# Two product groups moved onto banks already in use, and one weight block scaled earlier, in the channel half of a decoder layer

## The chip, the cores and the metric

The kernel runs on one core of a Trainium2 chip. The metric is the device time of one execution in microseconds. Four engines compute: PE (TensorE, the matrix engine, with its weight loads shown as PEld), DVE (VectorE), ACT (ScalarE) and POOL (GpSimd). SP (SyncE) only issues transfers. PE writes its results into PSUM, eight banks of 128 x 512 float32, from where DVE and ACT read them; everything else lies in SBUF, and weights come by DMA from device memory.

## The reference

One decoder layer on 512 tokens of width 1024: two attention branches, then a gated MLP, each followed by a LayerNorm. The change lies in the MLP:

```python
u2 = x * (1.0 + sc2) + sh2
h = _causal_depthwise_conv(u2 @ w_up, conv_w, conv_b)
h_gate, h_val = jnp.split(h, 2, axis=-1)
ffn_out = (jax.nn.silu(h_gate) * h_val) @ w_down
x = _layer_norm(DEEPNORM_ALPHA * x + (1.0 + gt2) * ffn_out, ln2_g, ln2_b)
```

Here `x` is 512 x 1024, `w_up` 1024 x 5632, `w_down` 2816 x 1024, and `(1.0 + gt2)`, called the gate below, is one factor per output column.

## The kernel before

**Split products.** Every float32 operand is split into a high part (ACT rounds it) and a low part (DVE subtracts the high part). A product is three matmuls: high x high, high x low, low x high. For streamed weights the high part is `wh` and the low part `wl` (`split_proc`, three buffers each) or, in the down projection's other blocks, `wdh` and `wdl`. The subtraction is line 91, whatever it works for.

**Up projection** (loop at line 1099, n = 0 to 43). Each n streams a weight tile of 128 x 1024, multiplies it with all tokens into one bank in 24 matmuls (lines 133 to 135), and applies the convolution: one ACT operation (line 1124) and two on DVE (lines 1125 and 1126) that read the bank. Six of the eight banks are held by running sums from n = 7 on, so two rotate here. Two tiles make one gated hidden tile, two hidden tiles make a pair; there are FP = 11 pairs.

**Down projection.** It is computed by the Strassen-Winograd scheme with seven products instead of eight for 2 x 2 blocks. The tokens are cut into two halves of 256 (the first half is row blocks 0 and 1 of 128 tokens, the second row blocks 2 and 3), the 1024 output columns into two halves of 512, and a pair's two hidden tiles are the inner halves. `blocks` (line 1051) forms sums of the activations on DVE. The weights of a pair are B11, B12, B21, B22 (each 128 x 512), and their sums are built in `pair_proc` (line 940): a transfer that adds gives the tile `b`, which holds T1 = B11 + B12 and T3 = B12 + B22, and two additions on DVE give T2 and T4. `b` is stored to device memory (`t13`) for later, and B22 times the gate's right half is stored too (`wgt`, written from tile `g`; the gate isn't ready for pairs 0 and 1, whose B22 is loaded and scaled at n = 15 and 19 by `scale_proc`).

A product of a pair is six matmuls, three for each of two row blocks (`product`, lines 1076 to 1078), and sums over the 11 pairs in two banks. The seven products and their place:

- P1 (with B11), Y (T2) and Z2 (T4) are summed during the up projection, pair by pair, in the six held banks (`early_products`).
- Z (T3) and W1 (T1) come after it, in two new banks each (`phase`), weights loaded back from `t13`.
- X (B21) and then W (B22, scaled) follow, again in two new banks each. W's first three pairs use `wl` weights; its last eight (`LATE`) are split ahead into `wdh`/`wdl`. For row block 2 these eight are one piece of 512 columns (24 matmuls, the wide piece), for row block 3 two pieces of 256 columns (24 narrow matmuls each), so that row block 3 can be normalised sooner.

**From products to output.** Between the matmuls DVE combines the products, multiplies by the gate's half `g0` or `g1` and adds to the residual `r[i][e]` (row block i, column half e; tiles `xn`). `gated` (line 1155) is the last two of these steps. `z_mark`, `v_mark`, `x_mark` and `w_mark` are called after each weight tile of the stages Z, W1, X and W and hold this work. P1 is first copied by ACT into `p1`. `tail` normalises a row block (`ln_stats`, then two scalings per piece, lines 1169 and 1173) and stores it.

**Order.** SP's loads stand in the order in which the program is written. On PE, DVE, ACT and POOL a scheduler sets the order when the program is built; each engine then works its list strictly in order, and waits on the others through semaphores. Weight items are loaded up to five ahead (`weights`).

Of the kernel before, what the change touches and what calls it, by code (L numbers as in the profile page):

```python
# [37 lines left out]
AHEAD = 2  # L38
NSPLIT = 3
LATE = 8  # L40
EARLY = 2
GS = 9
SS = 10
# [7 lines left out]
def layer_kernel(ctx: ExitStack, tc: tile.TileContext, out, xT, x, cT, crow, wa0, wa1, bcol, bgt, w1, wct, wv, bf,  # L51
# [912 lines left out]

    wui, pi, wai = [], [], {}
# [9 lines left out]
    for n in range(2 * FT):  # L975
        wui.append(add_item(wup[n], split_proc))
        if n in GTILES:
            k = GTILES.index(n)
            wai[(10, 28)[k // 4]] = add_item(wa1[(28, 24)[k // 4] + k % 4], ada_proc((28, 24)[k // 4] + k % 4))
        if n in (15, 19):  # L980
            p = (15, 19).index(n)
            add_item(wdp[p][:, 1024:1536], scale_proc(p), 512)
# [92 lines left out]
    def product(ps, ah, al, bh, bl, first, last):  # L1075
        PE.matmul(ps, ah, bh, start=first, stop=False)  # L1076
        PE.matmul(ps, ah, bl, start=False, stop=False)  # L1077
        return PE.matmul(ps, al, bh, start=False, stop=last)  # L1078

    yz = []  # L1080

# [70 lines left out]
    def half(w, e):  # L1152
        return [t[:, e * 512 : (e + 1) * 512] for t in w]

    def gated(i, e, t, src, op=ALU.add):
        V.tensor_tensor(t, src, (g0, g1)[e], ALU.mult)
        V.tensor_tensor(r[i][e], r[i][e], t, op)


    def stat_tile():  # L1160
        return cons.tile([P, 3, 6], F32, name=nm("st"), tag="st3", bufs=2)
# [11 lines left out]
            V.scalar_tensor_tensor(v, v, rs, lnr[1][:, c], ALU.mult, ALU.add)  # L1173
            eng.dma_start(out[tb, c], v)

    p1, u2, q1, u3, c22 = [[fine(n) for _ in range(2)] for n in ("p1", "u2", "q1", "u3", "c22")]

    def phase(ps, idx, end, take, mark, last=None):
        for n, k in enumerate(idx):
            w = weights(k)  # L1180
            for a, p in enumerate(range(2 * n, min(end, 2 * n + 2))):
                t = take(p)
                for i in range(2):
                    product(ps[i], t[:, top[i]], t[:, bot[i]], *half(w, a), p == 0, p == FP - 1)
            mark(n)
        if end < FP:
            t = take(end)
# [11 lines left out]
    def z_mark(n):  # L1199
# [3 lines left out]
        if n == 2:  # L1203
            early_products(FP - 1)
        if n == 3:
            Y, Z2, P1 = yz
            for i in range(2):
                S.activation(p1[i], P1[i], AF.Copy)
            for i in range(2):
                V.tensor_tensor(u2[i], p1[i], Y[i], ALU.subtract)  # L1210
# [5 lines left out]
    def v_mark(n):  # L1216
        for p in range(max(SS, 2 * n), min(FP, 2 * n + 2)):
            ops[p][3] = halves(ops[p][3])
        if n == 0:
            for i in range(2):  # L1220
                V.tensor_tensor(q1[i], q1[i], Z[i], ALU.add)
                V.tensor_tensor(u3[i], u2[i], Z[i], ALU.add)
        if n in (1, 2):
            gated(n - 1, 0, q1[n - 1], q1[n - 1])

    def first_rows(i):
        st = stat_tile()
# [2 lines left out]
        tail(i, st, [(0, 0, 512), (1, 0, 512)], G)  # L1230

    def x_mark(n):
        if n == 0:
            for i in range(2):
                V.tensor_tensor(c22[i], u3[i], W1[i], ALU.add)
                V.tensor_tensor(u2[i], u2[i], W1[i], ALU.add)
# [33 lines left out]
    V.tensor_tensor(r[3][1], r[3][1], W[1], ALU.add)  # L1270
    for i in range(2):
        pieces = [(1, 0, 512)] if i == 0 else [(1, 0, 256), (1, 256, 512)]
        for n, (e, c0, c1) in enumerate(pieces):
            ps = bank()[:, 0 : c1 - c0] if i else W[0]
            for q in range(LATE):
                t = ops[FP - LATE + q][3]
                product(ps, t[:, top[i]], t[:, bot[i]], wc[q][0][:, c0:c1], wc[q][1][:, c0:c1], i == 1 and q == 0, q == LATE - 1)
            v = r[2 + i][e][:, c0:c1]
            V.tensor_tensor(v, v, ps, ALU.add)
            V.bn_stats(sts[i][:, n + 1, :], v)  # L1280
        tail(2 + i, sts[i], [(0, 0, 512)] + pieces, nc.sync)

# [70 lines left out]
```

## Time and profile before

| what | value |
| --- | --- |
| median of 3 runs | 755.78 us (755.17 to 755.9) |
| profiled execution, its own time | 754.3 us |
| span of its instructions | 752.5 us |
| up projection on PE, about | 390 to 674 us |
| stages Z, W1, X, W on PE, about | 674 to 741 us |
| DMA over the span | 169 GB/s |

A row of the timeline gives start and length in microseconds, the engine, the line, the operation, output and inputs, shapes, how often, and in brackets the idle time before it and what ended it. Operations on one engine overlap at their ends, so the distance between two starts is what an operation costs its engine, not its length. A list of waits gives total, number and longest. "SPq" and "ACTq" are those engines' issues of transfers.

### The profile page before, as it was taken

The numbers are of one execution on the slowest core, as the hardware profiler recorded it, in microseconds if no ns is written. First come the engines' busy times: TensorE is split into PE (matmuls) and PEld (weight loads), VectorE is DVE, ScalarE is ACT, GpSimd is POOL, SyncE is SP. The second block draws the span as 40 slices with busy tenths as digits, with TensorE's granted clock in tenths as the row PEclk, the third lists the DMA queues.
The fourth block names the chain that finished last, engine by engine and source line by source line (L and its number), as shares of the span: only waits on it lengthen the run. The fifth ranks groups of instructions, "written<-read, shape, count | busy, mean of one in ns | idle before, by whom it ended". The sixth has DMA issues, their size and how long they took to land.

```text
span 752.5 us, 9875 instructions
## 1 busy us (share of the span) xinstructions
PE 734.0 (98%) x3478; PEld 607.6 (81%) x3478; DVE 607.1 (81%) x1017; ACT 386.0 (51%) x678; POOL 109.0 (14%) x138
## 2 busy tenths in 40 slices
PE   8999999999999999999999999999999999999993
PEld 4878888878888888788889888888888888887883
DVE  6869799888788894765587889987696678769997
ACT  4566566685866564433065554454454355346530
POOL 1026223453010011453000000000000000000010
PEclk9999999999999999999999999999999999999997
DMA  8943446313422331542063778587874665557611
GB/s 331 405 175 116 164 169 214 122 58 112 169 92 83 108 112 62 195 168 84 1 240 77 252 243 275 161 250 223 253 213 165 187 218 151 171 182 264 220 63 57
DMA packets 43252, 128.01 MB, mean 170 GB/s; under 512 B 5665, under 2 KB 6177, under 8 KB 43202
## 3 DMA queue, kind: packets, MB, share of 16 engines
q1 hardware_dynamic: 37602, 112.09, 42.5%
q0 software_dynamic: 2576, 7.41, 5.2%
q10 hardware_dynamic: 3024, 7.88, 3.0%
q8 instruction: 27, 0.44, 0.2%
q14 instruction: 23, 0.19, 0.1%
HBM read 117.07 MB, written 10.22 MB: 169 GB/s over the span
## 4 chain that ended last, share of the span: by engine, by line
PE 82%; DVE 10%; DMA 3%; issue 2%; ACT 2%; POOL 0%; SPq 0%; DVEq 0%; ACTq 0%
PE ps L135 18%; PE ps L133 18%; PE ps L134 18%; PE ps L301 5%; PE ps L1077 3%; PE ps L1078 2%; PE ps L1076 2%; PE ps L552 2%; DVE wl L91 2%; PE ps L534 2%; PE ps L893 2%; PE ps L892 2%; PE ps L894 2%; PE ps L475 1%; PE ps L476 1%
## 5 line engine op out<-in xcount | busy, mean ns | idle before, releaser
L91 DVE TENSOR_TENSOR wl<-raw,wh 128x1024 fp32r<-128x1024 f32 (+2 forms) x112 | 139.2, 1244 | 53.9 <-ACT wh L182 53.5
L182 ACT ACTIVATE wh<-raw 128x1024 fp32r<-128x1024 f32 (+1 forms) x103 | 108.5, 1053 | 124.0 <-PE ps L134 59.8
L133 PE MATMUL ps<-u2h,wh 128*128 128x512 f32 (+1 forms) x376 | 141.6, 377 | 0.0
L135 PE MATMUL ps<-u2h,wl 128*128 128x512 f32 (+1 forms) x376 | 141.2, 376 | 0.0
L134 PE MATMUL ps<-u2l,wh 128*128 128x512 f32 (+1 forms) x376 | 141.2, 376 | 0.0
L133 PEld LDWEIGHTS ps<-u2h,wh 128*128 128x128 f32 x376 | 70.8, 188 | 13.6 <-issue 0.8
L135 PEld LDWEIGHTS ps<-u2h,wl 128*128 128x128 f32 x376 | 70.8, 188 | 12.8
L134 PEld LDWEIGHTS ps<-u2l,wh 128*128 128x128 f32 x376 | 70.8, 188 | 12.7
L133 PE MATMUL ps<-uh,wh 128*128 128x512 f32 x200 | 79.4, 397 | 0.0
L135 PE MATMUL ps<-uh,wl 128*128 128x512 f32 x200 | 78.3, 391 | 0.9 <-DVE wl L91 0.9
L134 PE MATMUL ps<-ul,wh 128*128 128x512 f32 x200 | 78.3, 391 | 0.0
L1124 ACT ACTIVATE cv<-ps,cw 128x512 f32<-128x512 f32 x44 | 33.9, 770 | 24.9 <-PE ps L135 19.0
L135 PEld LDWEIGHTS ps<-uh,wl 128*128 128x128 f32 x200 | 37.6, 188 | 9.5 <-DVE wl L91 1.3
L161 POOL DMA_DIRECT2D raw<-in_wdp x11 | 9.5, 867 | 244.1 <-DVE raw L947 95.0
L514 POOL TENSOR_TENSOR pt<-pt,om 128x127 f32<-128x127 f32 (+3 forms) x32 | 43.2, 1360 | 8.0 <-DVE om L513 8.0
L133 PEld LDWEIGHTS ps<-uh,wh 128*128 128x128 f32 x200 | 37.6, 188 | 7.4
L134 PEld LDWEIGHTS ps<-ul,wh 128*128 128x128 f32 x200 | 37.6, 188 | 7.2
L1125 DVE SCALAR_TENSOR_TENSOR cv<-ps,cw,cv 128x511 f32<-128x511 f32 x44 | 32.8, 745 | 9.1 <-ACT cv L1124 9.1
L1132 ACT ACTIVATE cv<-cv 128x512 f32<-128x512 f32 x22 | 13.9, 630 | 39.0 <-DVE cv L1126 38.9
L1126 DVE SCALAR_TENSOR_TENSOR cv<-ps,cw,cv 128x510 f32<-128x510 f32 x44 | 32.8, 745 | 0.2
L633 POOL TENSOR_TENSOR raw<-raw,gt 128x1024 f32<-128x1024 f32 x8 | 20.9, 2618 | 66.9 <-DMA raw<-in_wo 54.4
L513 DVE TENSOR_TENSOR_SCAN om<-om,dg 128x127 f32<-128x127 f32 (+3 forms) x32 | 29.6, 982 | 0.5 <-ACT om L508 0.4
(226 smaller groups left out, 1607.3 us busy)
## 6 DMA issues: line engine op xcount, KB each, us to landing
raw<-in_wup SPq DMA_DIRECT2D x44, 512.0 KB, 4.6
raw<-in_wa SPq DMA_DIRECT2D x32, 512.0 KB, 4.3
raw<-in_wct SPq DMA_DIRECT2D x25, 512.0 KB, 3.7
raw<-in_wdp SPq DMA_DIRECT2D x22, 512.0 KB, 5.7
wa<-in_wa SPq DMA_DIRECT2D x14, 512.0 KB, 7.9
raw<-in_wdp SPq DMA_DIRECT2D x22, 256.0 KB, 4.6
raw<-in_wdp POOLq DMA_DIRECT2D x11, 512.0 KB, 7.7
t<-raw ACTq DMA_DIRECT2D x10, 512.0 KB, 3.6
```

The costliest lines, as they stand in the source:

```text
L91: state["read"] = V.tensor_tensor(o, i, fl(hi), ALU.subtract)
L133: PE.matmul(ps, wh, ah, start=first, stop=False)
L134: PE.matmul(ps, wh, al, start=False, stop=False)
L135: return PE.matmul(ps, wl, ah, start=False, stop=last)
L182: state["hi"] = S.activation(h[:, 0:cols], r[:, 0:cols], AF.Copy)
L301: PE.matmul(grp[g], w, u, start=j == 0 and n == 0, stop=j == KT - 1 and n == (1 if g == 7 else 2))
L513: V.tensor_tensor_scan(d0, d0, dg[:, 513 - (e - s) : 512][:, ::-1], 0.0, ALU.mult, ALU.max)
L514: G.tensor_tensor(pt[b][:, s : e - 1], pt[b][:, s : e - 1], om[:, s + 1 : e], ALU.mult)
L1077: PE.matmul(ps, ah, bl, start=False, stop=False)
L1124: S.activation(t, ps, AF.Identity, bias=cw[:, n, 3:4], scale=cw[:, n, 2:3])
L1125: V.scalar_tensor_tensor(t[:, 1:], ps[:, 0:511], cw[:, n, 1:2], t[:, 1:], ALU.mult, ALU.add)
L1126: V.scalar_tensor_tensor(t[:, 2:], ps[:, 0:510], cw[:, n, 0:1], t[:, 2:], ALU.mult, ALU.add)
```

## The change

1. **X goes on in P1's banks.** X's first matmul no longer clears a bank (`fresh=False`); it adds to P1, which ACT has copied before. P1 + X is then in the bank as the sum that the left half of the second token half needs, and one addition per row block is dropped in `w_mark`.
2. **W goes on in W1's banks.** Since W carries the gate's right half, W1 has to carry it too: T1 is multiplied by it in `pair_proc` before it is stored (pairs 2 to 10), and for pairs 0 and 1 the stored T1 is loaded, scaled and stored again at n = 23 and 27. DVE subtracts W1 from the residual of row blocks 0 and 1 before W begins, and W1 + W from that of row blocks 2 and 3 at the end. The sign of one activation sum (`s4`) is turned.
3. **The combinations between are written anew**: 24 DVE operations of 128 x 512 instead of 30, more of them in stages Z and W1 (`z_mark`, `v_mark`), fewer in X and W (`x_mark`, `w_mark`).

```diff
@@ pair_proc
             w = wdc_proc(r)
+            if p > 1:
+                V.tensor_tensor(b[:, 0:512], b[:, 0:512], gt[1][:, 512:1024], ALU.mult)
             with tc.issue_after(state["last"].ins):
                 if p < FP - 1:
                     S.dma_start(t13[p], b)
@@
-    def scale_proc(p):
+    def scale_proc(dst):
         def f(r):
             V.tensor_tensor(r, r, gt[1][:, 512:1024], ALU.mult)
-            G.dma_start(wgt[p], r)
+            G.dma_start(dst, r)
@@
+        if n in (23, 27):
+            t = t13[(23, 27).index(n)][:, 0:512]
+            add_item(t, scale_proc(t), 512)
@@ blocks
-        V.tensor_tensor(s4, o[:, hi], e[:, lo], ALU.subtract)
+        V.tensor_tensor(s4, e[:, lo], o[:, hi], ALU.subtract)
@@ z_mark
             for i in range(2):
                 V.tensor_tensor(u2[i], p1[i], Y[i], ALU.subtract)
-                V.tensor_tensor(q1[i], u2[i], Z2[i], ALU.add)
+        if n in (4, 5):
+            fold(n - 2, 1, tm[n - 4], u2[n - 4], ALU.subtract)
@@ v_mark
-        if n == 0:
-            for i in range(2):
-                V.tensor_tensor(q1[i], q1[i], Z[i], ALU.add)
-                V.tensor_tensor(u3[i], u2[i], Z[i], ALU.add)
-        if n in (1, 2):
-            gated(n - 1, 0, q1[n - 1], q1[n - 1])
+        if n in (0, 1):
+            for a, b, c in zip((u3, q1)[n], (u2, u3)[n], (Z, Z2)[n]):
+                V.tensor_tensor(a, b, c, ALU.add)
+        if n in (2, 3):
+            fold(n - 2, 0, q1[n - 2], q1[n - 2])
+        if n in (4, 5):
+            fold(n - 4, 1, u3[n - 4], u3[n - 4], ALU.subtract)
@@ x_mark
-        if n == 0:
-            for i in range(2):
-                V.tensor_tensor(c22[i], u3[i], W1[i], ALU.add)
-                V.tensor_tensor(u2[i], u2[i], W1[i], ALU.add)
-        if n in (1, 2):
-            gated(n - 1, 1, c22[n - 1], c22[n - 1], ALU.subtract)
-        if n in (3, 4):
-            first_rows(n - 3)
-        if n == 4:
-            for i in range(2):
-                gated(2 + i, 1, u2[i], u2[i], ALU.subtract)
+        if n in ROWS:
+            i = ROWS.index(n)
+            V.tensor_tensor(r[i][1], r[i][1], W1[i], ALU.subtract)
+            first_rows(i)
@@
-    X = [bank() for _ in range(2)]
-    phase(X, xi, FP, lambda p: ops[p][1], x_mark)
-    W = [bank() for _ in range(2)]
+    phase(P1, xi, FP, lambda p: ops[p][1], x_mark, fresh=False)
@@ w_mark
-                V.tensor_tensor(p1[i], p1[i], X[i], ALU.add)
-                gated(2 + i, 0, p1[i], p1[i])
+                fold(2 + i, 0, p1[i], P1[i])
@@
-                product(W[i], t[:, top[i]], t[:, bot[i]], *half(w, a), p == 0, i == 1 and p == FP - LATE - 1)
+                product(W1[i], t[:, top[i]], t[:, bot[i]], *half(w, a), False, i == 1 and p == FP - LATE - 1, True)
@@
-            ps = bank()[:, 0 : c1 - c0] if i else W[0]
+            ps = bank()[:, 0 : c1 - c0] if i else W1[0]
@@
-            V.tensor_tensor(v, v, ps, ALU.add)
+            V.tensor_tensor(v, v, ps, ALU.subtract)
```

`fold` is `gated` under another name, `ROWS` is (3, 4), and `product` gets a flag that allows sums to go on in a used bank.

The scheduler also places some instructions elsewhere. First, the end of PE's list. Before, W's first two matmuls (banks 6826 and 6827) are followed by all 48 narrow ones (banks 6896 and 6923), and the list ends with 16 more of W and the 24 of the wide piece, whose last rows are these:

```order
L1077 MATMUL ps_6826<-wdl_6732,hv_6206 128x512
L1078 MATMUL ps_6826<-wdh_6731,hv_6206 128x512
L1076 MATMUL ps_6826<-wdh_6772,hv_6639 128x512
L1077 MATMUL ps_6826<-wdl_6773,hv_6639 128x512
L1078 MATMUL ps_6826<-wdh_6772,hv_6639 128x512
```

Now W is in banks 6536 and 6537 (those of W1). After W's first two matmuls come 15 narrow ones of bank 6903, then the 16 of W and the wide piece, which ends in the first rows here, and then the narrow ones that are left:

```order
L1082 MATMUL ps_6536<-wdh_6786,hv_6660 128x512
L1083 MATMUL ps_6536<-wdl_6787,hv_6660 128x512
L1084 MATMUL ps_6536<-wdh_6786,hv_6660 128x512
L1082 MATMUL ps_6903<-wdh_6720,hv_6014 128x256
L1083 MATMUL ps_6903<-wdl_6721,hv_6014 128x256
L1084 MATMUL ps_6903<-wdh_6720,hv_6014 128x256
```

So 9 matmuls of bank 6903 and 24 of bank 6930 moved from ahead of the wide piece to behind it; these three kinds of rows go on to the list's end.

Second, the end of DVE's list, where `xn_3625`/`xn_3626` are row block 2's column halves and `xn_3741`/`xn_3742` row block 3's. Before:

```order
L1270 TENSOR_TENSOR xn_3742<-xn_3742,ps_6827 128x512
L1279 TENSOR_TENSOR xn_3742<-xn_3742,ps_6896 128x256
L1279 TENSOR_TENSOR xn_3742<-xn_3742,ps_6923 128x256
L1280 BN_STATS st_6829<-xn_3742 128x6 x2
L1279 TENSOR_TENSOR xn_3626<-xn_3626,ps_6826 128x512
L1280 BN_STATS st_6828<-xn_3626 128x6
L854 BN_AGGR mv_6883<-st_6828 128x2
L854 BN_AGGR mv_6950<-st_6829 128x2
```

Now:

```order
L1276 TENSOR_TENSOR xn_3626<-xn_3626,ps_6536 128x512
L1277 BN_STATS st_6837<-xn_3626 128x6
L1276 TENSOR_TENSOR xn_3742<-xn_3742,ps_6903 128x256
L855 BN_AGGR mv_6890<-st_6837 128x2
L1277 BN_STATS st_6838<-xn_3742 128x6
L858 TENSOR_SCALAR mv_6890<-mv_6890 128x1
L859 RECIPROCAL mv_6890<-mv_6890 128x1
L1174 SCALAR_TENSOR_TENSOR xn_3625<-xn_3625,mv_6890,ln_0_5279 128x512
```

Row block 2 is added and normalised first, the four scalings of lines 1174 and 1178 included, and only then comes row block 3's second narrow piece (bank 6930) with its own normalisation.

Third, DVE's list in stage X. Before, two operations per row block read W1 near the stage's start:

```order
L91 TENSOR_TENSOR wdl_6679<-rl_6644,wdh_6678 128x512
L1235 TENSOR_TENSOR c_1178_6321<-u_1176_6319,ps_6517 128x512
L1236 TENSOR_TENSOR u_1172_6315<-u_1172_6315,ps_6517 128x512
L1235 TENSOR_TENSOR c_1179_6322<-u_1177_6320,ps_6518 128x512
L1236 TENSOR_TENSOR u_1173_6316<-u_1173_6316,ps_6518 128x512
L91 TENSOR_TENSOR wl_6683<-raw_6646,wh_6682 128x1024
```

Now one operation per row block reads it, row block 1's behind the first scalings of row block 0:

```order
L92 TENSOR_TENSOR wl_6749<-raw_6717,wh_6748 128x1024
L1241 TENSOR_TENSOR xn_3490<-xn_3490,ps_6536 128x512
L1235 BN_STATS st_6765<-xn_3489 128x6
L1235 BN_STATS st_6765<-xn_3490 128x6
L92 TENSOR_TENSOR wdl_6787<-rl_6740,wdh_6786 128x512
L855 BN_AGGR mv_6768<-st_6765 128x2
```

Four operations at X's start became two late in it, and they are now the last readers of W1 before W writes those banks.

More of the change, by code (lines that the diff above doesn't have):

```diff
@@ L40 @@
 LATE = 8
+ROWS = (3, 4)
 EARLY = 2
@@ L981, in layer_kernel @@
             p = (15, 19).index(n)
-            add_item(wdp[p][:, 1024:1536], scale_proc(p), 512)
+            add_item(wdp[p][:, 1024:1536], scale_proc(wgt[p]), 512)
+        if n in (23, 27):
+            t = t13[(23, 27).index(n)][:, 0:512]
+            add_item(t, scale_proc(t), 512)
         if n >= 5 and n % 4 == 1 and n < 2 * FT - 2:
@@ L1073, in blocks, with product @@
         yield
[L1075 to L1078, printed above, removed]
+    def product(ps, ah, al, bh, bl, first, last, onto=False):
+        PE.matmul(ps, ah, bh, start=first, stop=False, skip_group_check=onto)
+        PE.matmul(ps, ah, bl, start=False, stop=False, skip_group_check=onto)
+        return PE.matmul(ps, al, bh, start=False, stop=last, skip_group_check=onto)
     yz = []
@@ L1153, in half, with fold @@
         return [t[:, e * 512 : (e + 1) * 512] for t in w]
-    def gated(i, e, t, src, op=ALU.add):
+    def fold(i, e, t, src, op=ALU.add):
         V.tensor_tensor(t, src, (g0, g1)[e], ALU.mult)
@@ L1174, in tail, with phase @@
             eng.dma_start(out[tb, c], v)
-    p1, u2, q1, u3, c22 = [[fine(n) for _ in range(2)] for n in ("p1", "u2", "q1", "u3", "c22")]
-    def phase(ps, idx, end, take, mark, last=None):
+    p1, u2, q1, u3, tm = [[fine(n) for _ in range(2)] for n in ("p1", "u2", "q1", "u3", "tm")]
+    def phase(ps, idx, end, take, mark, last=None, fresh=True):
         for n, k in enumerate(idx):
@@ L1183, in phase @@
                 for i in range(2):
-                    product(ps[i], t[:, top[i]], t[:, bot[i]], *half(w, a), p == 0, p == FP - 1)
+                    product(ps[i], t[:, top[i]], t[:, bot[i]], *half(w, a), fresh and p == 0, p == FP - 1, not fresh)
             mark(n)
@@ L1205, in z_mark @@
         if n == 3:
-            Y, Z2, P1 = yz
             for i in range(2):
@@ L1232, in x_mark @@
     def x_mark(n):
[L1233 to L1243 removed]
+        if n in ROWS:
+            i = ROWS.index(n)
+            V.tensor_tensor(r[i][1], r[i][1], W1[i], ALU.subtract)
+            first_rows(i)
+    Y, Z2, P1 = yz
     lnr = lnr2
@@ L1266, in layer_kernel @@
             for i in range(2):
-                product(W[i], t[:, top[i]], t[:, bot[i]], *half(w, a), p == 0, i == 1 and p == FP - LATE - 1)
+                product(W1[i], t[:, top[i]], t[:, bot[i]], *half(w, a), False, i == 1 and p == FP - LATE - 1, True)
         w_mark(n)
     wc = [weights(k) for k in cli]
-    V.tensor_tensor(r[3][1], r[3][1], W[1], ALU.add)
+    V.tensor_tensor(r[3][1], r[3][1], W1[1], ALU.subtract)
     for i in range(2):
@@ L1273, in layer_kernel @@
         for n, (e, c0, c1) in enumerate(pieces):
-            ps = bank()[:, 0 : c1 - c0] if i else W[0]
+            ps = bank()[:, 0 : c1 - c0] if i else W1[0]
             for q in range(LATE):
                 t = ops[FP - LATE + q][3]
-                product(ps, t[:, top[i]], t[:, bot[i]], wc[q][0][:, c0:c1], wc[q][1][:, c0:c1], i == 1 and q == 0, q == LATE - 1)
+                product(ps, t[:, top[i]], t[:, bot[i]], wc[q][0][:, c0:c1], wc[q][1][:, c0:c1], i == 1 and q == 0, q == LATE - 1, i == 0)
             v = r[2 + i][e][:, c0:c1]
-            V.tensor_tensor(v, v, ps, ALU.add)
+            V.tensor_tensor(v, v, ps, ALU.subtract)
             V.bn_stats(sts[i][:, n + 1, :], v)
```

## The prediction

> **What bounds the kernel now.** I began with the page's first part, then went to the list of TensorE's waits.
>
> ```profile
> span 752.5 us, 9875 instructions
> PE 734.0 (98%) x3478; PEld 607.6 (81%) x3478; DVE 607.1 (81%) x1017; ACT 386.0 (51%) x678; POOL 109.0 (14%) x138
> ...
> PE ps L193 <- DMA cbr<-in_crow: 2.2, 1, 2.2
> PE ps L1077 <- DVE wl L91: 0.9, 1, 0.9
> PE ps L1077 <- DVE wdl L91: 0.3, 1, 0.3
> ```
>
> TensorE (PE) is busy for 98% of the span, and the change neither adds nor removes a matmul. So it can win only what PE does not work: the single wait of 0.9 us at line 1077, and the time behind the last matmul. It can lose wherever VectorE (DVE), which it gives other work, makes PE wait. The table of stretches tells how much room DVE has: two from the up projection, then the stages Z, W1, X, W and the end.
>
> ```profile
> 468.00:494.00 26.00, 26.00 (x117) 21.38 (x116) 24.29 (x41) 11.05 (x19) 1.44 (x2) 1.00 0.64 194
> 520.00:546.00 26.00, 26.00 (x116) 21.52 (x116) 17.75 (x30) 12.95 (x22) 0.86 (x1) 1.00 0.77 248
> ...
> 674.00:694.60 20.60, 20.14 (x85) 15.45 (x84) 18.13 (x31) 13.28 (x23) 0.00 (x0) 1.00 0.69 236
> 694.60:709.60 15.00, 15.00 (x68) 12.43 (x67) 15.00 (x22) 8.33 (x12) 0.00 (x0) 1.00 0.66 221
> 709.60:724.50 14.90, 14.90 (x67) 12.35 (x66) 14.90 (x28) 7.46 (x11) 0.00 (x0) 1.00 0.29 97
> 724.50:741.20 16.70, 15.75 (x91) 13.51 (x89) 15.25 (x31) 0.29 (x1) 2.23 (x4) 1.00 0.17 63
> ```
>
> The columns are the stretch, its length, then busy time of PE, PEld, DVE, ACT and POOL, the granted clock, and the DMA. In W1 and X both PE and DVE are busy all the time, and only in W does PE lose anything. The clock is 1.00 throughout, so I leave it out. PE's own rows show what happens in W, where ps is the bank written:
>
> ```profile
> 709.56 0.39 PE L1076 MATMUL ps<-wh,hv 128*128 128x512 f32 x1
> 709.79 0.39 PE L1077 MATMUL ps<-wl,hv 128*128 128x512 f32 x1
> ...
> 724.52 0.62 PE L1076 MATMUL ps<-wh,hv 128*128 128x512 f32 x2
> 724.97 0.28 PE L1076 MATMUL ps<-wdh,hv 128*128 128x256 f32 x1
> 725.09 0.28 PE L1077 MATMUL ps<-wdl,hv 128*128 128x256 f32 x1
> ...
> 730.61 0.28 PE L1078 MATMUL ps<-wdh,hv 128*128 128x256 f32 x1
> 731.78 0.50 PE L1077 MATMUL ps<-wl,hv 128*128 128x512 f32 x1 [0.90 <-DVE wl L91]
> ...
> 740.76 0.39 PE L1078 MATMUL ps<-wdh,hv 128*128 128x512 f32 x1
> ```
>
> X's 66 matmuls take 709.56 to 724.52, so a 512-wide one costs 0.227 us; a 256-wide one costs 0.12. At 724.52 the first two W products start, and then W's low weights (wl) are missing. Its 48 narrow matmuls for the last 128 rows fill 5.76 us of the hole, and 0.9 us stays open. The missing wl comes from DVE, which is late:
>
> ```profile
> 692.26 0.69 DVE L1210 TENSOR_TENSOR u<-p,ps 128x512 f32<-128x512 f32 x1
> 693.66 0.43 DVE L91 TENSOR_TENSOR hv<-sg,hv 128x256 fp32r<-128x256 f32 x1 [0.71 <-ACT hv L88]
> ...
> 709.62 0.68 DVE L1235 TENSOR_TENSOR c<-u,ps 128x512 f32<-128x512 f32 x1
> 710.21 0.68 DVE L1236 TENSOR_TENSOR u<-u,ps 128x512 f32<-128x512 f32 x1
> ...
> 730.51 1.22 DVE L91 TENSOR_TENSOR wl<-raw,wh 128x1024 fp32r<-128x1024 f32 x1
> 731.65 0.68 DVE L1157 TENSOR_TENSOR xn<-xn,u 128x512 f32<-128x512 f32 x1
> ```
>
> From 693.66 on, DVE's rows follow each other without a gap: it is a queue, and every operation taken out ahead of 730.51 brings this wl forward. Starts lie 0.60 apart for a 128x512 operation and 1.14 for a wl of 1024 columns. Behind the last matmul DVE works alone:
>
> ```profile
> 738.36 0.75 DVE L1279 TENSOR_TENSOR xn<-xn,ps 128x256 f32<-128x256 f32 x2
> 739.02 0.75 DVE L1280 BATCH_NORM_STATS2 st<-xn 128x6 f32<-128x256 f32 x2
> 741.19 0.69 DVE L1279 TENSOR_TENSOR xn<-xn,ps 128x512 f32<-128x512 f32 x1 [1.42 <-PE ps L1078]
> 741.91 0.69 DVE L1280 BATCH_NORM_STATS2 st<-xn 128x6 f32<-128x512 f32 x1
> 742.64 0.31 DVE L854 BATCH_NORM_AGGREGATE mv<-st 128x2 f32<-128x12 f32 x2
> ...
> 745.32 1.41 DVE L1173 SCALAR_TENSOR_TENSOR xn<-xn,mv,ln 128x512 f32<-128x512 f32 x2
> 746.64 0.22 DVE L859 SCALAR_TENSOR_TENSOR mv<-mv 128x1 f32<-128x1 f32 x1
> ...
> 747.64 1.54 DVE L1173 SCALAR_TENSOR_TENSOR xn<-xn,mv,ln 128x512 f32<-128x512 f32 x3
> 746.10 3.62 SPq L1174 DMA_DIRECT2D out<-xn  x5
> ```
>
> Since the wide piece of rows 256 to 383 is PE's last, the normalisation of both remaining row blocks comes after it: 741.15 to 749.18, 8.0 us. Then the last store's issue, landing and the end of the program take 3.3 us to 752.5.
>
> **The change part by part.** *Up projection.* Nine multiplications of T1 and two more for the first two pairs: 11 x 0.60 = 6.6 us of DVE work, two loads and two stores of 256 KB. PE works 26.00 of 26.00 us in both stretches above, and DVE idles between 470 and 674:
>
> ```profile
> DVE wl L91 <- ACT wh L182: 30.9, 16, 6.3
> DVE cv L1125 <- ACT cv L1124: 8.7, 6, 4.1
> ...
> raw<-in_wdp SPq DMA_DIRECT2D x22, 256.0 KB, 4.6
> ```
>
> Those idle 39.6 us are waits for high parts that ACT cannot write before PE has freed a weight buffer, so the weights run ahead as far as the buffers allow. 6.6 us spread over 200 us fits. The price on the path lies between 0 and 6.6 us; I take 0. If the cover were gone, every multiplication would cost PE 0.6. ACT's store of T1 now waits for the product, but the order puts that directly behind the sums, beside ACT's second wdh, so ACT loses some 0.1 us per pair at half load. The 256 KB loads, 4.6 us each, stand in SP's queue ahead of one up-projection weight each; they take no raw buffer and what they read was stored long before.
>
> *Stage Z.* Pair 10's extra 0.6 us sits between its first two wdl, but a wl of 1.14 us moves behind the second: that wdl comes 0.5 earlier, the two of T1 and T3 come 0.6 later and the wl 1.2, which W1 needs only at 694.60. Bounds -0.3 to +0.6, taken as 0.
>
> *W1 and X: DVE's queue.* Counting the changed order from the first u (692.26) through W's first wl: 28 operations of 128x512 (20 of them arithmetic on the results, 8 wdl), 9 wl of 1024, one of 512, two hv, 4 statistics, 4 scalings and a few tiny ones: 28 x 0.60 + 9 x 1.14 + 0.6 + 2 x 0.33 + 4 x 0.60 + 4 x 0.66 + 0.5 = 33.9 us, hence 726.2 instead of 731.65. The wait of 0.71 for ACT's hv also goes, since three other operations now stand ahead of it.
>
> The work moved forward must not starve PE on the way. Adding up the same order, W1's fourth wl (11 x 0.60 + 0.33 + 2 x 1.14 behind 692.26) is done at 701.5 and wanted at 694.60 + 37 x 0.227 = 703.0; X's second (another 11 x 0.60 + 0.33 + 3 x 1.14) is done at 711.9 and wanted at 709.56 + 13 x 0.227 = 712.5. These two, 1.5 and 0.6 us, are the thin places. Cost between 0 and 1.5 us; I take 0.
>
> *The new wait.* PE may write B22 into W1's banks only after DVE has read both. By the same sum the second read ends at 722.4, behind the statistics of row block 0; PE comes at 724.75. Cost 0, with 2.3 us to spare; behind that matmul stand all of W and the end. P1's banks are read by ACT's copy, which the first u (692.26) uses, 17 us before X begins, so X waits for nothing. The Trainium skill ("PSUM — Partial Sum Buffer", "PSUM bank collisions raise a hardware error") says that no two engines may touch one bank at a time and a semaphore has to keep them apart; by it, sharing can only add a wait, and no run here shows a collision; by the 2.3 us that wait is empty.
>
> *The end.* PE issues two W products and 15 narrow matmuls to 724.97 + 1.8 = 726.77, when wl (726.2) is there. Then 16 more W products and the 24 of the wide piece: 40 x 0.227 = 9.1, issue done at 735.85, result about 0.16 later, 736.0 instead of 741.15. The other 33 narrow ones follow, to 739.8 + 0.16 = 740.0.
>
> DVE from 736.0: add and statistics of the wide piece 0.72 each, first narrow add and statistics 2 x 0.36, four scalings at 0.66, tiny ones 0.5: 5.3 us, to 741.3. So PE's last matmul is hidden. Then the last narrow piece: add and statistics 0.42 each, aggregate and tiny ones 0.6, two 512-wide scalings 1.32, four 256-wide 1.6: 4.4 us, to 745.7 instead of 749.18. The last store stays as it was.
>
> **Sum:** 0 + 0 + 0 - 3.5 = -3.5 us. The span goes from 752.5 to 749.0, the profiled execution from 754.3 (1.8 us around the span) to 750.8. The median of the runs shown, 755.78, is 1.5 above the profiled one; the same 3.5 below it is 752.3.
>
> **Rivals.** *Thin places tear.* One wait of DVE like the 0.71 us above, ahead of 712, delays X's second wl and so PE; two such cost 1.5 us. For it: W1 and X without any slack in DVE. Against it: that wait had its cause in ACT's place in the queue, and the order has taken DVE past it. Gain 2.0, time 753.8.
>
> *The wide piece is not earlier by much.* If W's wl came only 2 us earlier instead of 5.4, PE would stand after its 15 narrow matmuls (1.8 us of cover instead of 5.76), the wide piece would end near 739.0, and 9.7 us of DVE work behind it would end at 748.7: gain 0.5, time 755.3. For it: ACT now writes W's wh behind the square root of row block 0, so a late step there holds this wl. Against it: W's wh was done 8.8 us before its wl began:
>
> ```profile
> 720.64 1.07 ACT L182 ACTIVATE wh<-raw 128x1024 fp32r<-128x1024 f32 x1 [2.09 <-PE ps L1078]
> ```
>
> *Slower: the multiplications reach PE through the up projection's banks.* Only two banks rotate there, and tile n+2 waits for the last convolution step of tile n:
>
> ```profile
> 548.48 0.74 DVE L1126 SCALAR_TENSOR_TENSOR cv<-ps,cw,cv 128x510 f32<-128x510 f32 x1
> ...
> 549.52 0.40 PE L133 MATMUL ps<-u2h,wh 128*128 128x512 f32 x1
> ```
>
> The bank is free at 549.22 and taken at 549.52. If each of the 11 multiplications delayed such a release with no slack, PE would lose 6.6 us: 752.3 + 6.6 = 758.9; the sixth uses up the gain of 3.5. Against it: at 468 to 494, the fullest stretch, DVE still has 1.7 us, the delay comes once in some 26 us, and in the changed order this convolution step stands ahead of the wl it now waits behind.
>
> **How the numbers follow.** Forecast 0.70 (751.2 to 753.3), thin places 0.14, wide piece not earlier 0.08, slower 0.08. A difference under 0.2%, 1.5 us, can't be told from none. Faster: 0.70 + 0.14 = 0.84; same 0.08; slower 0.08. The range takes in the second case and leaves out the last two: 750.8 to 754.8.
>
> **What would show it.** In the changed profile: the rows of PE's narrow matmuls split 15 and 33, the wide piece ahead of the 33, no wait of 0.9 us at the first W product; DVE's W wl near 726; the second read of W1 before 724; DVE without a gap from some 736 to 746; no PE wait between 470 and 674. The forecast is wrong if PE waits for wl or for W1's read between 700 and 727 by over 1.5 us, or if its matmuls in the up projection lose their 0.227 us step.

## The result, and the profile after

The changed kernel was compared with the one before three times:

| comparison | before, us (range, runs) | changed, us (range, runs) | ratio | 95% interval |
| --- | --- | --- | --- | --- |
| first | 755.47 (754.58 to 756.43, 6) | 751.85 (751.11 to 752.74, 6) | 0.9953 | 0.994 to 0.9966 |
| second | 754.72 (752.78 to 755.43, 10) | 752.2 (751.81 to 752.64, 6) | 0.997 | 0.9959 to 0.9981 |
| third | 754.54 (753.43 to 755.82, 21) | 752.09 (751.08 to 754.36, 12) | 0.9972 | 0.9963 to 0.9981 |

It is faster, by 3.6 us in the first comparison and by 2.5 us in the other two. The profiled execution of the changed kernel took 752.35 us, its span 750.6. The page's first lines and the list of PE's waits now read:

```profile
span 750.6 us, 9886 instructions
PE 734.2 (98%) x3478; PEld 608.0 (81%) x3478; DVE 610.7 (81%) x1022; ACT 386.2 (51%) x678; POOL 109.8 (15%) x140
```

```profile
PE ps L1084 <- DVE hv L92: 0.6, 1, 0.6
...
PE ps L1083 <- DVE wdl L92: 0.2, 1, 0.2
```

(The file has grown: the low-part subtraction is now line 92, `product` is lines 1082 to 1084, the two scalings of `tail` are lines 1174 and 1178.) PE's wait for W's `wl`, 0.9 us before, is gone. In its place stands a wait that the kernel before did not have: 0.6 us for a low half of the activations (`hv`), at line 1084. The table of stretches, with the columns explained above, puts it in stage Z:

```profile
468.00:494.00 26.00, 26.00 (x117) 21.51 (x116) 23.13 (x41) 11.06 (x19) 1.44 (x2) 1.00 0.62 190
520.00:546.00 26.00, 26.00 (x116) 21.56 (x115) 21.61 (x36) 13.63 (x22) 1.43 (x2) 1.00 0.80 258
674.00:694.60 20.60, 19.65 (x83) 15.03 (x82) 18.17 (x31) 12.97 (x23) 0.00 (x0) 1.00 0.67 218
694.60:709.60 15.00, 15.00 (x67) 12.41 (x67) 15.00 (x23) 7.44 (x10) 0.00 (x0) 1.00 0.70 231
709.60:724.50 14.90, 14.90 (x67) 12.35 (x66) 14.61 (x25) 8.54 (x11) 0.00 (x0) 1.00 0.40 120
724.50:741.20 16.70, 16.70 (x98) 14.75 (x96) 14.88 (x33) 1.22 (x3) 2.23 (x4) 1.00 0.17 63
```

PE is busy without a gap in the up projection, although DVE does more there (21.61 us instead of 17.75 in the second stretch), and in W1, X and W. Only 674 to 694.6 lost: 19.65 us instead of 20.14. DVE's rows at the end, in the timeline of the changed kernel:

```profile
723.38 0.66 DVE L1241 TENSOR_TENSOR xn<-xn,ps 128x512 f32<-128x512 f32 x1
...
726.79 1.17 DVE L92 TENSOR_TENSOR wl<-raw,wh 128x1024 fp32r<-128x1024 f32 x1
...
735.05 0.66 DVE L1267 TENSOR_TENSOR xn<-xn,ps 128x512 f32<-128x512 f32 x1
737.48 0.69 DVE L1276 TENSOR_TENSOR xn<-xn,ps 128x512 f32<-128x512 f32 x1 [1.76 <-PE ps L1084]
...
741.47 1.41 DVE L1178 SCALAR_TENSOR_TENSOR xn<-xn,mv,ln 128x512 f32<-128x512 f32 x2
742.80 0.41 DVE L1276 TENSOR_TENSOR xn<-xn,ps 128x256 f32<-128x256 f32 x1
...
745.88 1.54 DVE L1178 SCALAR_TENSOR_TENSOR xn<-xn,mv,ln 128x512 f32<-128x512 f32 x3
```

From top to bottom: the second read of W1; W's `wl`, done at 727.96 instead of 731.73; DVE ready for the wide piece and waiting 1.76 us for it; the wide piece's addition at 737.48 instead of 741.19; row block 2's last scalings; the last narrow piece, which is in PSUM since about 741.4 and is added at 742.80, as soon as DVE has time; the last scalings, done at 747.42 instead of 749.18. PE's rows around the first W products and at the end:

```profile
725.94 0.61 PE L1082 MATMUL ps<-wh,hv 128*128 128x512 f32 x2
726.39 0.28 PE L1082 MATMUL ps<-wdh,hv 128*128 128x256 f32 x1
...
728.18 0.40 PE L1083 MATMUL ps<-wl,hv 128*128 128x512 f32 x1
...
741.11 0.28 PE L1084 MATMUL ps<-wdh,hv 128*128 128x256 f32 x1
```

Two W products, 15 narrow ones, and then `wl`, written at 727.96 and used at 728.18. The last matmul is a narrow one.

### The profile page after: what moved, and what is told of

The parts are those of the page before. It is cut to its first block, busy times and chain, and to the rows that moved or that the text cites. A ratio compares the mean times of both kernels' runs of the same rounds, so it can differ in the third digit from the quotient of the medians.

```text
span 750.6 us, 9886 instructions
## 1 busy us (share of the span) xinstructions
PE 734.2 (98%) x3478; PEld 608.0 (81%) x3478; DVE 610.7 (81%) x1022; ACT 386.2 (51%) x678; POOL 109.8 (15%) x140
## 4 chain that ended last, share of the span: by engine, by line
PE 86%; DVE 7%; DMA 3%; ACT 2%; issue 1%; POOL 0%; SPq 0%; DVEq 0%; ACTq 0%
PE ps L136 18%; PE ps L134 18%; PE ps L135 18%; PE ps L302 5%; PE ps L1084 4%; PE ps L1082 4%; PE ps L1083 4%; PE ps L553 2%; PE ps L535 2%; PE ps L895 2%; PE ps L893 2%; PE ps L894 2%; DVE wl L92 1%; PE ps L476 1%; PE ps L477 1%
## 5 line engine op out<-in xcount | busy, mean ns | idle before, releaser
L92 DVE TENSOR_TENSOR wl<-raw,wh 128x1024 fp32r<-128x1024 f32 (+2 forms) x112 | 139.2, 1244 | 39.6 <-ACT wh L183 39.3
```

The lines of the kernel that those rows point to most:

```text
L92: state["read"] = V.tensor_tensor(o, i, fl(hi), ALU.subtract)
```

## The experiments

Three questions were open. Is the gain at the end due to the order of PE's matmuls, to the shorter DVE queue, or to both? Do the scaled T1 and the shared banks cost anything? And does DVE or PE set the end now? Twelve runs follow, two of them the changed kernel again as a measure beside the others ("r_after_again" and "r_after_third", rows two and three of the table above).

> The changed kernel itself, on the chip of the runs that follow, as their measure. By its first comparison (ratio 0.9953, 0.994 to 0.9966) 3.0 to 4.5 us below the kernel before. If the difference here is under 2 us, the gain belongs to that chip's pairing and not to the change.

> The changed kernel a third time, as the measure for the three runs that follow it and for the size of the gain, of which two comparisons gave 3.6 and 2.5 us. Expected between these, 2.5 to 3.6 us below the kernel before.

Both gave 2.5 us: less than the 3.0 to 4.5 expected of the first, and the lower edge of what was expected of the second. Of the 1.1 us that the first comparison shows beyond that, 0.3 lies in the changed kernel and 0.8 in the kernel before.

**Only the order of the matmuls (e1).** The kernel before, with the wide piece and W ahead of 33 narrow matmuls as in the changed kernel.

```diff
-                product(ps, t[:, top[i]], t[:, bot[i]], wc[q][0][:, c0:c1], wc[q][1][:, c0:c1], i == 1 and q == 0, q == LATE - 1)
+                with ExitStack() as behind:
+                    if i == 1 and (n or q > 4):
+                        behind.enter_context(tc.issue_after(wide.ins))
+                    m = product(ps, t[:, top[i]], t[:, bot[i]], wc[q][0][:, c0:c1], wc[q][1][:, c0:c1], i == 1 and q == 0, q == LATE - 1)
+            if i == 0:
+                wide = m
```

> The kernel before, with nothing changed but the end of TensorE's list: as in the changed kernel, 15 narrow matmuls stand ahead of the rest of W and of the wide piece, the other 33 behind it. Theory (the order pays only because W's low weights come earlier): they still come at 731.7, TensorE stands idle from 726.8 to 731.8, the wide piece ends at 741.1 as before, and 9.7 us of VectorE work behind it instead of 8.0 end 1.6 us later: 757.1 us. Rival (the order alone is the gain): 3.5 us faster than before, 752.0 us.

758.16 us (757.66 to 759.13, 5 runs) against 754.73 (754.0 to 756.19, 23 runs): ratio 1.0048, 1.0036 to 1.006, slower by 3.4 us. The order alone is a loss; it pays only where DVE's `wl` comes earlier. Why it lost twice the 1.6 us that were expected shows in PE's rows of this run:

```profile
731.61 0.79 PE L1077 MATMUL ps<-wl,hv 128*128 128x512 f32 x1 [5.08 <-DVE wl L91]
732.21 0.63 PE L1078 MATMUL ps<-wh,hv 128*128 128x512 f32 x1
732.63 0.63 PE L1077 MATMUL ps<-wl,hv 128*128 128x512 f32 x1
...
735.11 0.40 PE L1077 MATMUL ps<-wl,hv 128*128 128x512 f32 x1
735.35 0.39 PE L1078 MATMUL ps<-wh,hv 128*128 128x512 f32 x1
```

PE stands for 5.08 us, and its next matmuls start 0.42 to 0.43 us apart instead of 0.227, until about 735. The granted clock of that stretch says the same (the third number from the end):

```profile
731.60:736.00 4.40, 4.39 (x12) 3.54 (x13) 4.40 (x8) 0.00 (x0) 0.00 (x0) 0.61 0.00 0
```

The eight steps from 731.61 to 735.11 took 3.50 us where eight of 0.227 take 1.82, 1.7 us lost. PE also went on 0.2 us earlier than in the kernel before (731.61 against 731.78), and in all the wide piece is added 1.4 us later (742.58 instead of 741.19). Behind it DVE has 9.9 us of work (to 752.52) instead of 8.0:

```profile
742.58 0.69 DVE L1284 TENSOR_TENSOR xn<-xn,ps 128x512 f32<-128x512 f32 x1 [4.43 <-PE ps L1078]
```

The 1.4 and the 1.9 make 3.3 of the 3.4 us. Only the second had been expected, as 1.6.

**Only the shorter queue (e2).** The changed kernel with all 48 narrow matmuls ahead of W again and the wide piece last. `piece(i, n)` is the loop over the eight pairs' products of one piece.

```diff
...
+    for n in range(2):
+        narrow = piece(1, n)
     for n, k in enumerate(wi):
         w = weights(k)
+        with tc.issue_after(narrow.ins):
...
+            if i == 0:
+                with tc.issue_after(narrow.ins):
+                    piece(0, 0)
...
```

> The changed kernel with all 48 narrow matmuls ahead of W, so that the wide piece comes last as before. Theory (earlier low weights and the new order give the gain together): only the 0.9 us wait and some tenths go, the wide piece ends at 740.0 instead of 741.1 and 8.0 us of VectorE work follow: 1.2 us faster than before, 754.3 us. Rival (the shorter VectorE queue alone is the gain, the order is incidental): as the changed kernel, 751.9 us.

753.76 us (753.32 to 754.96, 11 runs): ratio 0.9986, 0.9977 to 0.9994, faster than before by 1.0 us. DVE's rows:

```profile
741.98 0.69 DVE L1287 TENSOR_TENSOR xn<-xn,ps 128x512 f32<-128x512 f32 x1 [3.30 <-PE ps L1084]
...
748.43 1.53 DVE L1178 SCALAR_TENSOR_TENSOR xn<-xn,mv,ln 128x512 f32<-128x512 f32 x3
```

The tail is back to 8.0 us behind the wide piece (741.98 to 749.96), with DVE idle for 3.3 us ahead of it. W's wait of 0.9 us is gone, but the new wait in stage Z is here too:

```profile
693.02 0.50 PE L1084 MATMUL ps<-wdh,hv 128*128 128x512 f32 x1 [0.62 <-DVE hv L92]
```

From stage Z's row with `fo` (shown under e3 below) to PE's last matmul it is 50.68 us here, 50.94 in the kernel before and 50.78 in the changed one, so these two nearly cancel. This trace accounts for 0.3 of the 1.0 us; where the rest comes from stays open. The shorter queue alone does not shorten the tail; the order that it permits does, from 8.42 us behind the start of the last matmul (8.41 in e2) to 6.31.

**Without the scaling of T1 (e3).** The multiplications in `pair_proc` and the two items at n = 23 and 27 are left out, so that W1 lacks its gate.

```diff
-            if p > 1:
-                V.tensor_tensor(b[:, 0:512], b[:, 0:512], gt[1][:, 512:1024], ALU.mult)
...
-        if n in (23, 27):
-            t = t13[(23, 27).index(n)][:, 0:512]
-            add_item(t, scale_proc(t), 512)
```

> The changed kernel without the 11 multiplications of T1 and without the two loads and stores that go with them; T1 is left unscaled, so W1 lacks the gate. Theory (they are hidden under TensorE but for stage Z, where the trace of the changed kernel shows a new wait of 0.6 us): 751.3 to 751.9 us. Rival (each reaches TensorE): 6.6 us less, 745.3 us.

752.1 us (751.04 to 753.06, 5 runs), ratio 0.9962, 0.995 to 0.9974: as the changed kernel, and not the 751.3 to 751.9 expected. By the median the eleven multiplications cost nothing. The trace says more. In stage Z of this run there is no wait for `hv`. DVE's rows there, first of the kernel before, then of the changed one:

```profile
690.55 0.75 DVE L91 TENSOR_TENSOR hv<-cv,hv 128x256 fp32r<-128x256 f32 x2
```

```profile
688.47 0.68 DVE L951 TENSOR_TENSOR raw<-raw,gt 128x512 f32<-128x512 f32 x1
...
692.01 0.75 DVE L92 TENSOR_TENSOR hv<-cv,hv 128x256 fp32r<-128x256 f32 x2
...
693.69 1.27 DVE L1214 TENSOR_TENSOR u<-p,ps 128x512 f32<-128x512 f32 x2
```

and PE's rows that use this `hv`, in the same order:

```profile
689.82 0.40 PE L1078 MATMUL ps<-wdh,fo 128*128 128x512 f32 x1
...
691.20 0.39 PE L1078 MATMUL ps<-wdh,hv 128*128 128x512 f32 x1
691.43 0.39 PE L1077 MATMUL ps<-wdl,hv 128*128 128x512 f32 x1
```

```profile
690.33 0.40 PE L1084 MATMUL ps<-wdh,fo 128*128 128x512 f32 x1
...
691.48 0.39 PE L1082 MATMUL ps<-wdh,hv 128*128 128x512 f32 x1
692.48 0.50 PE L1084 MATMUL ps<-wdh,hv 128*128 128x512 f32 x1 [0.61 <-DVE hv L92]
692.82 0.39 PE L1083 MATMUL ps<-wdl,hv 128*128 128x512 f32 x1
```

The low half of the last pair's activations was ready a fraction of a microsecond ahead of PE. Pair 10's T1 multiplication (the row of line 951) now stands ahead of it. PE was 0.51 us behind the kernel before at the row with `fo` (690.33 against 689.82) and is 1.39 behind at the last row (692.82 against 691.43): 0.9 us lost. The step from `fo` to that row takes 2.49 to 2.52 us in all ten profiled executions in which pair 10's T1 is scaled, and 1.61 or 1.62 in the four in which it isn't (the kernel before, e1, e3, e4). In e3's own profiled execution another wait, of 0.65 us at 667.59, took most of the 0.9 us that were won. Its rows on ACT and PE:

```profile
667.12 0.72 ACT L89 ACTIVATE hv<-cv 128x256 fp32r<-128x256 f32 x2 [0.72 <-DMA wgt<-wg]
...
667.59 0.50 PE L1077 MATMUL ps<-wdh,hv 128*128 128x512 f32 x1 [0.65 <-ACT hv L89]
```

What ended ACT's idle time there is, by the row, the store of scaled B22. Whether e3 has this wait in every execution, or its median only varies by as much, stays open.

**Only X on P1's banks (e4).** The kernel before with this part of the change alone.

```diff
...
-    X = [bank() for _ in range(2)]
-    phase(X, xi, FP, lambda p: ops[p][1], x_mark)
+    phase(P1, xi, FP, lambda p: ops[p][1], x_mark, fresh=False)
...
-                V.tensor_tensor(p1[i], p1[i], X[i], ALU.add)
-                gated(2 + i, 0, p1[i], p1[i])
+                gated(2 + i, 0, p1[i], P1[i])
```

> The kernel before with only the first part: X goes on in P1's banks, two VectorE additions are gone from the end of stage W. Theory (they stood behind W's low weights, where VectorE waits for the wide piece anyway): no change, 755.5 us within 0.4. Rival (this part shortens what bounds the end): 1.2 us faster, 754.3 us.

754.69 us (752.68 to 756.74, 12 runs): ratio 1.0001, 0.9992 to 1.0009. No change.

**X back in its own banks (e8).** The counterpart: the changed kernel without this part.

```diff
-    phase(P1, xi, FP, lambda p: ops[p][1], x_mark, fresh=False)
+    X = [bank() for _ in range(2)]
+    phase(X, xi, FP, lambda p: ops[p][1], x_mark)
...
-                fold(2 + i, 0, p1[i], P1[i])
+                V.tensor_tensor(p1[i], p1[i], X[i], ALU.add)
+                fold(2 + i, 0, p1[i], p1[i])
```

> The changed kernel with X back in two banks of its own: P1 and X are added on DVE again, two operations of 0.6 us behind W's first weight tile. All else stays, W on W1's banks, the scaled T1 and the matmul order. Theory (X's part is worth nothing, since the two additions lie ahead of the wide piece's sum, where DVE waits 1.76 us for PE): as the changed kernel within 0.5 us. Rival (X's part takes its share through the 1.2 us of DVE work that it saves): 0.8 to 1.2 us slower than the changed kernel.

751.57 us (751.24 to 753.77, 10 runs; ratio to before 0.9967, 0.9957 to 0.9977), beside 752.09 for the changed kernel: not slower. The wide piece's row on DVE tells why:

```profile
736.67 0.69 DVE L1278 TENSOR_TENSOR xn<-xn,ps 128x512 f32<-128x512 f32 x1 [0.55 <-PE ps L1084]
```

The two more operations (1.2 us) came out of DVE's 1.76 us of idle time, which is 0.55 here. X's part of the change is worth nothing in the time, alone or with the rest.

**W in its own banks (e10).** The changed kernel, but PE need not wait for DVE's reading of W1; W1 and W are subtracted one by one.

```diff
+    W = [bank() for _ in range(2)]
...
+                V.tensor_tensor(r[2 + i][1], r[2 + i][1], W1[i], ALU.subtract)
                 fold(2 + i, 0, p1[i], P1[i])
...
-                product(W1[i], t[:, top[i]], t[:, bot[i]], *half(w, a), False, i == 1 and p == FP - LATE - 1, True)
+                product(W[i], t[:, top[i]], t[:, bot[i]], *half(w, a), p == 0, i == 1 and p == FP - LATE - 1)
...
```

> The changed kernel with W in two banks of its own, so that its first matmul does not wait until DVE has read W1; row blocks 2 and 3 then subtract W1 and W separately, two more DVE operations of 0.6 us ahead of the wide piece's sum. The order of PE stays. Theory (the wait on W1's read is empty, and DVE has 1.76 us free there): as the changed kernel within 0.5 us. Rival (the wait on the shared banks holds W back): 0.6 us or more faster than the changed kernel.

751.75 us (751.33 to 752.16, 5 runs; ratio 0.9964, 0.9952 to 0.9976), 0.3 us below the changed kernel: the wait on the shared banks is empty. In the changed kernel the second read ends at 724.04 (723.38 and 0.66 above) and PE's first W product starts at 725.94.

**Row block 2's second scaling off DVE (e6), and left out (e9).** Both ask whether DVE or PE sets the end.

```diff
...
-            V.scalar_tensor_tensor(v, v, rs, lnr[1][:, c], ALU.mult, ALU.add)
+            if off:
+                S.activation(v, v, AF.Copy, scale=rs)
+                G.tensor_tensor(v, v, lnr[1][:, c], ALU.add)
+            else:
+                V.scalar_tensor_tensor(v, v, rs, lnr[1][:, c], ALU.mult, ALU.add)
...
```

(`off` is true for row block 2 alone, and so is `skip` below.)

> The changed kernel with row block 2's second scaling (x times rs plus b, two operations of 0.66 on DVE) done by ACT (times rs) and POOL (plus b) instead. Theory (DVE's queue behind the wide piece, and not PE's last matmul, sets the end: row block 2 is done 1.7 us after the last matmul's result in the changed kernel's trace): the end comes 1.0 to 1.3 us earlier. Rival (PE's last matmul sets the end, or POOL's additions slow DVE): no change within 0.4 us, or slower.

e6: 752.08 us (751.72 to 752.38, 5 runs; ratio 0.9968, 0.9956 to 0.9981), beside 752.2 for the changed kernel. No change, as the rival said. Its rows on POOL and DVE show which of the rival's two reasons:

```profile
741.30 2.92 POOL L1180 TENSOR_TENSOR xn<-xn,ln 128x512 f32<-128x512 f32 x2 [9.90 <-ACT xn L1179]
741.72 1.39 DVE L1174 SCALAR_TENSOR_TENSOR xn<-xn,mv,ln 128x512 f32<-128x512 f32 x1
743.10 1.41 DVE L1174 SCALAR_TENSOR_TENSOR xn<-xn,mv,ln 128x256 f32<-128x256 f32 x1
744.56 0.47 DVE L1174 SCALAR_TENSOR_TENSOR xn<-xn,mv,ln 128x256 f32<-128x256 f32 x1
```

While POOL adds (741.30 to 744.22), DVE's 512-wide scaling takes 1.39 us instead of 0.74 and a 256-wide one 1.41 instead of 0.47, 1.6 us more for the 1.3 saved; once POOL is done, the next takes 0.47 again. The Trainium skill ("SBUF — State Buffer", "Who interferes with whom") says that a DVE instruction with two SBUF inputs and a GpSimd instruction that reads SBUF exclude each other, the later one standing until the other is through, and that a DVE instruction with one SBUF input, outside the faster two-port modes, is not affected. The trace agrees: the two slow scalings, with `xn` and `ln` in SBUF, end 0.55 and 0.29 us after POOL's first and second addition (at 742.56 and 744.22), and POOL's second addition, which meets the first of them, takes 1.70 us where the other takes 1.26.

The same edit without POOL settles it. In e9, row block 2's output lacks the second scaling altogether, that is the factor `rs` and the bias.

```diff
...
-            V.scalar_tensor_tensor(v, v, rs, lnr[1][:, c], ALU.mult, ALU.add)
+            if not skip:
+                V.scalar_tensor_tensor(v, v, rs, lnr[1][:, c], ALU.mult, ALU.add)
...
```

> The changed kernel without row blocks 2 and 3's second scaling of row block 2, that is without its two operations of 0.66 us on DVE and with nothing in their place (row block 2's output is then only x minus the mean, times nothing). Theory (DVE's queue behind the wide piece sets the end by up to 1.3 us, and the run in which ACT and POOL did this scaling lost it again because DVE's scalings took twice as long beside POOL): 1.0 to 1.4 us below the changed kernel. Rival (PE's last matmul sets the end, POOL's presence is beside the point): no change within 0.4 us.

750.55 us (750.02 to 751.2, 5 runs; ratio 0.9948, 0.9936 to 0.996), 1.5 us below the changed kernel. In the trace it is 8.58 us from the wide piece's addition to the end of DVE's work (737.63 to 746.21) instead of 9.94, and DVE has no idle time in between. DVE's queue behind the wide piece sets the end of the changed kernel.

**The reads of W1 and row blocks 0 and 1 one weight tile later (e5).** One number differs:

```diff
-ROWS = (3, 4)
+ROWS = (4, 5)
```

The scheduler then puts all of W and the wide piece ahead of all 48 narrow matmuls.

> The changed kernel with W1's two reads and row blocks 0 and 1's normalisation one weight tile later in X (ROWS is (4, 5)). The order then puts all 16 remaining W products straight behind the first two, then the wide piece, then all 48 narrow matmuls, since W's low weights no longer stand behind row block 1's scalings. Theory (what stands behind the wide piece on DVE sets the end): wide piece's result some 1.8 us earlier (15 narrow matmuls of 0.12 less ahead of it), row block 2's add, statistics and four scalings (5.3 us) wholly beside PE's 48 narrow matmuls (5.8 us), so that only the last narrow piece's 4.4 us stand behind the last matmul: 1.3 to 1.8 us below the changed kernel. Rival (the second read of W1 is what counts): read later by 1 to 2 us than its 724.0, it makes PE wait at W's first matmul, which no narrow matmul can cover, and the time is 0 to 2 us above the changed kernel.

750.39 us (749.99 to 751.07, 5 runs): ratio 0.9948, 0.9936 to 0.9961, 4.3 us below the kernel before and 1.8 below the changed one beside it. DVE's rows:

```profile
721.74 0.67 DVE L1241 TENSOR_TENSOR xn<-xn,ps 128x512 f32<-128x512 f32 x1
...
724.75 1.23 DVE L92 TENSOR_TENSOR wl<-raw,wh 128x1024 fp32r<-128x1024 f32 x1
...
735.97 0.67 DVE L1276 TENSOR_TENSOR xn<-xn,ps 128x512 f32<-128x512 f32 x1
...
740.03 1.40 DVE L1178 SCALAR_TENSOR_TENSOR xn<-xn,mv,ln 128x512 f32<-128x512 f32 x2
741.45 0.42 DVE L1276 TENSOR_TENSOR xn<-xn,ps 128x256 f32<-128x256 f32 x1
```

W's `wl` comes 2 us earlier, the wide piece is added at 735.97, and row block 2 is done at 741.43, just when the last narrow piece is there. The rival had no test here: DVE's order, as the scheduler set it, reads W1 the second time at 721.74, not later but earlier than at 723.38. e10 is the run that answers it.

**Both (e7).** The number of e5 and the edit of e6.

> Both edits: the reads one tile later and row block 2's second scaling off DVE. Theory: once the wide piece comes 1.8 us earlier, the end hangs on PE's last matmul plus 4.4 us, so the second edit adds at most 0.4 us to the first: 1.3 to 2.0 us below the changed kernel, and not the sum of the two (2.3 to 3.1). Rival (both limits add): 2.3 to 3.1 us below.

750.48 us (750.05 to 750.85, 5 runs; ratio 0.9947, 0.9933 to 0.9961): like e5 alone. DVE now waits for the last narrow piece; POOL's additions, earlier here, still run when it comes:

```profile
739.80 2.50 POOL L1180 TENSOR_TENSOR xn<-xn,ln 128x512 f32<-128x512 f32 x2 [6.79 <-ACT xn L1179]
740.66 0.42 DVE L1280 TENSOR_TENSOR xn<-xn,ps 128x256 f32<-128x256 f32 x1 [1.31 <-PE ps L1084]
741.11 0.43 DVE L1281 BATCH_NORM_STATS2 st<-xn 128x6 f32<-128x256 f32 x1
```

DVE's 1.31 us of idle time make PE's last matmul the bound, so the two gains don't add. e5 is the version that beats both kernels, and by the smaller edit.

## Why the prediction came out as it did

**The mechanism was right.** The gain comes from the end: W's `wl` is early enough for the wide piece to go ahead of 33 narrow matmuls, and row block 2's normalisation then lies beside them. e1 and e2 show that neither half gives the whole gain alone (3.4 us slower and 1.0 us faster), and e9 that DVE's queue behind the wide piece is what ends last, as the sum had it.

**The parts that were right.** *Up projection, 0:* PE is busy for 284.00 of the 284.00 us from 390 to 674, and e3's median shows no gain without the multiplications. *W's `wl`, done at 726.2:* it was done at 727.96, but the queue from the first u (693.69) through it took 34.3 us, near the 33.9 worked out; it began 1.4 us late (below), and the `wl` still came 0.2 us ahead of PE. *Thin places:* no PE wait in W1 or X. *The read of W1:* 724.04 instead of 722.4, still 1.9 us ahead of PE. *DVE between the wide piece and the last narrow one, 5.3 us:* 737.48 to 742.80. *Split of the narrow matmuls, no wait of 0.9 us, no PE wait in the up projection:* as said. (Of the 39.6 us of idle time that the prediction calls waits for high parts, 8.7 are waits for ACT's convolution step; the sum doesn't use it.)

**The step that failed is stage Z, taken as 0.** It followed pair 10's multiplication to the `wdl` and to a `wl` that has time, but not to the `hv` halves behind them in the same queue, which PE took as soon as they were there. The bounds, -0.3 to +0.6, were too narrow: it cost 0.9 us. The first u, from which the queue of W1 and X was counted, stands behind those `hv` halves and comes later by the same 0.6 us of DVE work.

**A term of the tail was small by 0.2.** From the last narrow addition to the last scaling's end it is 4.62 us (742.80 to 747.42), not 4.4. The aggregate and the small operations took 0.73 us of it instead of 0.6; the rest is spread over the others.

**Why the sum still fits.** The two profiled executions part at their start, in code that is the same. PE's row there, before and after:

```profile
15.48 0.73 PE L301 MATMUL ps<-uh,wh 128*128 128x512 f32 x2
```

```profile
16.65 0.73 PE L302 MATMUL ps<-uh,wh 128*128 128x512 f32 x2 [0.87 <-ACT uh L268]
```

ACT was late once, as it is in some executions of the kernel before too: in e4's profile the same wait is there. Of these 1.17 us PE is still 0.51 late at the row with `fo` in stage Z. Then come +0.9 for `hv`, and -1.04 from there to the last matmul (741.11 against 740.76), most of it W's wait of 0.9. From the start of the last matmul to DVE's end it is 6.31 us instead of 8.42, -2.1. That is -1.76 at DVE's end and -1.9 in the span, or -2.3 at DVE's end if the 0.51 of late start is left out. Predicted were -1.1 for PE (the last narrow matmul, over at 739.8, starts at 739.7) and -2.4 for the tail, together -3.5: stage Z's 0.9 and some 0.3 of the tail are what it has too much. The 2.5 us of the second and third comparison fit the trace. That the first comparison gave 3.6 us, next to the 3.5 forecast, is luck: its median of the kernel before, 755.47, is 0.8 and 0.9 us above those of the other two. The forecast of 752.3 us for the time was carried in the same way, by a first median of 755.78.

**The rivals.** The thin places held. That the wide piece comes little earlier is refuted by its 3.7 us. That the multiplications reach PE through the up projection's banks is refuted by the same 284.00 us; one is shown to reach PE, pair 10's in stage Z. Whether the others have a part in a further wait stays open: in eight of the ten profiled executions with the scaled T1, but also in e4 without it, PE waits 0.3 to 0.5 us early in stage Z for the last convolution step on DVE (0.48 at 679.02 in the second comparison's profile). The profiled executions shown above, before and after, list no such wait.

## What to carry to other kernels

An order that puts long work first pays only where its inputs are there; move the queue of the engine that makes them first, and see that the wait stays short. When an operation is added to an engine's queue, follow everything that stands behind it to its user, and look for the user that takes it the moment it is done. Before work is moved to another engine, see what that engine's inputs share with the one relieved: in e6 the 1.3 us saved were lost again.

## What the hardware showed that was not expected

After 5.08 us without a matmul the next eight steps of PE take 3.50 us and not 1.82 (e1; granted clock 0.50 from 731.60 to 735.00 and 1.00 from 735.00 to 736.00), 1.7 us on top of the wait; the kernel before kept a clock of 1.00 around its wait of 0.9 us. The Trainium skill ("TensorE: Matmul & The Clock Gate", "Part 1: The HAM clock gate (the "warmup" mystery)") says that TensorE's clock is halved after an idle window of about 3.4 us and comes back after about as much sustained work. The trace agrees: the slow rows span 731.61 to 735.11, 3.5 us.

DVE's scalings with two operands in SBUF took up to three times as long beside POOL's additions (1.41 us instead of 0.47, e6), and one of POOL's additions 1.70 us instead of 1.26. Operations with one operand in SBUF did not: in e7's rows above an addition from PSUM and a statistics operation lie within POOL's two additions and take their usual 0.42 and 0.43 us.
